# One norm, early modulation products, two projections abreast, later sends and single PSUM banks in a two-layer hybrid backbone kernel

## The chip, the core and the metric

The kernel runs on one core of one Trainium2 chip. The core has five engines: TensorE (PE; its weight loads are listed as PEld), VectorE (DVE), ScalarE (ACT), GpSimd (POOL) and SyncE (SP), which only issues DMAs here; ScalarE issues some as well. Each engine works its own list of instructions in order and waits on semaphores for the others. The metric is the time of the whole program on the core in microseconds, the median of several runs.

## What is computed

The reference runs two layers over a latent stream x (512 tokens of 1024 channels) and a context stream (256 tokens). A layer is, cut to what matters here:

```python
mod = silu(c) @ ada_w[l] + ada_b[l]               # six vectors; c_ctx gives those of the context
h = rmsnorm(x, norm1_w[l]) * (1 + sc1) + sh1      # for both streams
cu, mqkv, mo, mg, aq, ak, av, bg = split(h @ w_in[l])
conv = conformer_conv(cu)                         # width 31, layer norm, projection
m = mlstm_readout(mlstm_bidirectional(mqkv, mg))  # 4 heads of 256, chunkwise, gates in float32
a = attention(aq, ak, av)                         # 8 query heads of 64 on 2 key heads, rotary
x = x + g1 * ((s0 * conv + s1 * m + s2 * a) @ w_out[l])
h = rmsnorm(x, norm2_w[l]) * (1 + sc2) + sh2
x = x + g2 * conv_ffn(h)                          # up, width-3 convolution, gate, down
```

The mLSTM's output is a numerator over max(|denominator|, exp(-m)). The context goes through layer 0 in full; in layer 1 it only gives keys, values and mLSTM states. The output is x, in float32.

## The kernel before

**Layout and products.** Tokens lie along the free dimension, channels on the 128 partitions, so a stream of T = 768 tokens (512 latent, then 256 context) is eight tiles of 128x768. A float32 product is made of three float32r matmuls: each weight block and each activation is split into a high and a low part, and hh·wh, hl·wh, hh·wl are summed in PSUM (accumulate, L664). Weights come as units of four 128x128 blocks in the order of use (class Weights, L188): SP loads a unit into a `raw` tile, ScalarE makes the high part wh (L215), POOL the low part wl (L217); conversions run up to two units ahead, loads five.

**Steps and ticks.** proj (L671) is a generator: one step is one k block of a projection (3 matmuls of 512 columns, and 3 of 256 where the context takes part). A Filler (L234) holds a queue of such generators; run(n) takes n steps from it, and after each step tick counts down the side chains that were handed to chain. A side chain yields a number of ticks that it wants to wait before its next piece is emitted. So the order in each engine's list is written by hand, and gaps in ticks are the distances between the pieces of a chain. drain empties the queue; settle runs the chains out with no steps between.

**The beginning** (L692 to L711). SP loads the eight xt tiles, then aw, the weights of the modulation vectors: ada_first (L436) has four parts of eight 128x512 pieces, (f, vec) with f the half of the channels and vec 1 the scale, 0 the shift. Three parts are loaded at once into buffers that later stages use (`room`), the fourth behind the first product, because its last two pieces take B buffers of the first. For the latent and then the context stream the squares of all eight blocks are summed (Norm.square, L592) and scale_early (L604) makes 1/rms by row sums on PE, a square root on ScalarE, a reciprocal on VectorE, and spreads it over the partitions by PE into PSUM, where VectorE multiplies all eight blocks. Then, for each half, two products (16 matmuls, a copy, four small transposes, an addition), factors (L611), and apply_scaled (L641): ScalarE scales and shifts a block into a t3 tile (a ring of three), VectorE rounds it to the high part hh, and VectorE or POOL takes the low part hl. The first weight unit is taken after all that.

**mLSTM heads** (L1206 to L1249). The gates' projection starts the chain mgates (L760), which ends with PE's L837. Each of four heads queues its projections (conv 16 steps, output gates, the next head's q, k, v: 72 steps) and emits at given steps, listed in HEADS and HEADS1 as `step:what`: D (decay: rows from DRAM, exponentials on ScalarE L1027), S (scores; VectorE multiplies, and denominators, L1058, adds up the columns in L1061), R (normalise, L1074), V (weights times values, L1183), s (split of the finished heads). The digit is the group of 256 queries. R makes row sums on PE (L545), takes Abs on ScalarE, a maximum and a reciprocal on VectorE, and sends the four rows back to all partitions with four DMAs on SP (send_rows, L534); norm_gap ticks later VectorE multiplies six score pieces by them (L1086). head_norm (L1130) sends its rows in the same way. The taps of the width-31 convolution (L924) run on VectorE, one every second step.

**Behind the heads** (L1295 to L1307) two mlstm_out projections are taken six steps far, one after the other, while the last head's chain ends; settle, and then the rest.

**Attention** (L1443 to L1511). Keys, values, one branch gate and three query chunks are queued, 48 steps; prepare(i) (L1377) of a head copies its query (L1383), and finds the maxima of its scores: PE L1396 and L1403 into a pv bank, VectorE L1397 and L1405, then a transpose L1413 and L1414. prepare(0) is chained after 24 steps, the queue is drained, the convolution's output projections and branch gates are queued, and the sweep runs over 64 (layer 0) or 48 (layer 1) items: attend(j) makes a block of scores and its exponentials, weigh(j) multiplies by values. prepare(i + 1) is chained when head i begins.

**PSUM.** Eight banks of 128x512: two mm tiles of 1024 columns (four banks), two sm and two pv tiles of one bank.

## Time and profile before

| | |
|---|---|
| median of 3 runs | 3086.83 us (3085.42 to 3087.39) |
| the profiled execution | 3092.18 us, its span 3090.4 us |
| PE busy | 2839.3 us (92% of the span) |
| PEld, DVE, ACT, POOL busy | 77%, 58%, 38%, 37% |
| mean granted TensorE clock | 0.972 |
| DMA | 262.48 MB, 85 GB/s over the span |
| chain that ended last | PE L668 11% of the span, all else 3% |

A busy share is the time in which an engine executes something. The granted clock is 1.00 at 2.4 GHz and 0.50 at 1.2 GHz; the first 78 us have no record of it and are shown as 1.00. In the lists of waits, a row names the waiting engine and line, then what ended the wait, the sum, how many and the longest. Layer 0 goes to about 1822 us, layer 1 from there.

### The profile page before, as it was taken

The page shows a single profiled execution, that of the slowest core. Times are in us where ns is not written, and L with a number is a line of the kernel's source. Part 1 is how long each engine was busy: PE and PEld are TensorE (multiplying, and loading weights), DVE is VectorE, ACT ScalarE, POOL GpSimd, SP SyncE. Part 2 cuts the span into 40 slices and gives each one's busy share as a digit, 9 for nine tenths or more (in the row PEclk, how much of TensorE's full clock was granted, in tenths as well). Part 3 has the DMA queues.
Part 4 walks back from the last instruction along what each step waited for, and adds up shares of the span by engine and source line. Part 5 has one row for each costly group of instructions (what it writes and reads, how often), then busy time and mean ns, then how long its engine had stood idle before and what let it go on. Part 6 is the DMA issues. An engine that isn't in the chain of part 4 may idle for free. (4 is left out here: it accounts for less than half of the span.)

```text
span 3090.4 us, 42030 instructions
## 1 busy us (share of the span) xinstructions
PE 2839.3 (92%) x15970; PEld 2387.5 (77%) x15970; DVE 1806.4 (58%) x2506; ACT 1164.5 (38%) x2136; POOL 1148.0 (37%) x931
## 2 busy tenths in 40 slices
PE   4999999899899998999999988999989789899999
PEld 2778888788677887888888877887767567777887
DVE  3366776852655335876665565778764663563444
ACT  3333333423444424322322353433434444443333
POOL 1233333323344434333332343334334345444444
PEclk9999999999899998999999989999999999999999
DMA  5454334211111133333333232333322112423333
GB/s 180 149 126 106 60 61 68 49 61 55 31 31 31 56 116 96 113 116 113 113 120 106 71 116 58 68 63 74 69 72 72 35 38 75 153 87 96 93 96 106
DMA packets 156682, 262.48 MB, mean 85 GB/s; under 512 B 17784, under 2 KB 37624, under 8 KB 156480
## 3 DMA queue, kind: packets, MB, share of 16 engines
q1 hardware_dynamic: 150048, 253.28, 29.5%
q10 hardware_dynamic: 6432, 6.52, 0.8%
q8 instruction: 126, 2.06, 0.3%
q14 instruction: 76, 0.62, 0.1%
HBM read 247.05 MB, written 5.46 MB: 82 GB/s over the span
## 5 line engine op out<-in xcount | busy, mean ns | idle before, releaser
L217 POOL TENSOR_TENSOR wl<-raw,wh 128x512 fp32r<-128x512 f32 x659 | 908.4, 1384 | 1516.4 <-ACT wh L215 1444.8
L668 PE MATMUL mm<-hh,wh 128*128 128x512 f32 (+1 forms) x2672 | 965.3, 361 | 21.9 <-ACT wh L215 8.8
L668 PE MATMUL mm<-hh,wl 128*128 128x512 f32 (+1 forms) x2672 | 949.3, 355 | 9.4 <-POOL wl L217 9.4
L668 PE MATMUL mm<-hl,wh 128*128 128x512 f32 (+1 forms) x2672 | 954.9, 357 | 2.0 <-POOL hl L346 1.2
L215 ACT ACTIVATE wh<-raw 128x512 fp32r<-128x512 f32 x662 | 411.1, 625 | 592.7 <-PE mm L668 328.8
L668 PEld LDWEIGHTS mm<-hh,wh 128*128 128x128 f32 x2672 | 513.7, 192 | 120.2 <-issue 23.5
L668 PEld LDWEIGHTS mm<-hh,wl 128*128 128x128 f32 x2672 | 511.5, 191 | 87.9 <-POOL wl L217 14.0
L668 PEld LDWEIGHTS mm<-hl,wh 128*128 128x128 f32 x2672 | 513.4, 192 | 70.8 <-POOL hl L346 1.8
L668 PE MATMUL mm<-C,wh 128*128 128x512 f32 (+1 forms) x1168 | 410.8, 352 | 0.3 <-DVE C L346 0.3
L668 PE MATMUL mm<-B,wh 128*128 128x512 f32 (+1 forms) x976 | 345.5, 354 | 29.2 <-DVE big L1542 15.0
L668 PE MATMUL mm<-B,wl 128*128 128x512 f32 (+1 forms) x976 | 342.9, 351 | 9.9 <-POOL wl L217 9.3
L924 DVE SCALAR_TENSOR_TENSOR AC<-G,par,AC 128x783 f32<-128x783 f32 (+1 forms) x240 | 258.5, 1077 | 3.8
L668 PEld LDWEIGHTS mm<-C,wh 128*128 128x128 f32 x1168 | 227.6, 195 | 28.6 <-DVE C L346 0.5
L668 PEld LDWEIGHTS mm<-B,wh 128*128 128x128 f32 x976 | 190.7, 195 | 61.2 <-ACT wh L215 14.5
L668 PEld LDWEIGHTS mm<-B,wl 128*128 128x128 f32 x976 | 190.1, 195 | 37.8 <-POOL wl L217 14.6
L1592 DVE SCALAR_TENSOR_TENSOR AC<-mm,par,AC 128x511 f32<-128x511 f32 (+1 forms) x132 | 86.7, 657 | 205.1 <-ACT AC L1590 205.1
L1542 DVE SCALAR_TENSOR_TENSOR big<-mm,mod,big 128x512 f32<-128x512 f32 (+1 forms) x144 | 91.1, 657 | 122.9 <-PE mm L668 122.8
L1590 ACT ACTIVATE AC<-mm,par 128x768 f32<-128x768 f32 (+1 forms) x88 | 77.4, 879 | 145.7 <-PE mm L668 145.5
L346 POOL TENSOR_TENSOR P<-t,P 128x512 fp32r<-128x512 f32 (+1 forms) x64 | 73.4, 1148 | 132.3 <-ACT t L1473 75.7
L488 DVE SCALAR_TENSOR_TENSOR P<-C,cs,P 128x512 f32<-128x512 f32 x112 | 114.7, 1056 | 1.5 <-DMA C<-aw 1.5
L1027 ACT ACTIVATE C<-rb,bias 128x128 f32<-128x128 f32 x312 | 96.4, 390 | 35.7 <-DMA rb<-rows 23.2
L1111 PE MATMUL pv<-P,C 128*128 128x256 f32 x624 | 95.9, 291 | 8.0 <-DVE P L346 6.6
(270 smaller groups left out, 3735.8 us busy)
## 6 DMA issues: line engine op xcount, KB each, us to landing
raw<-ws SPq DMA_DIRECT2D x662, 256.0 KB, 2.6
C<-aw SPq DMA_DIRECT2D x104, 256.0 KB, 3.1
big<-aw SPq DMA_DIRECT2D x64, 256.0 KB, 4.2
P<-ws SPq DMA_DIRECT2D x30, 256.0 KB, 2.8
big<-xt SPq DMA_DIRECT2D x16, 384.0 KB, 6.6
rb<-rows ACTq DMA_DIRECT2D x40, 128.0 KB, 4.0
den<-rd SPq DMA_DIRECT2D x80, 64.0 KB, 5.8
B<-aw SPq DMA_DIRECT2D x10, 256.0 KB, 6.5
```

Source lines behind the costliest of these rows:

```text
L215: self.nc.scalar.activation(out=hi, in_=raw, func=AF.Copy)
L217: eng.tensor_tensor(out=lo, in0=raw, in1=hi.bitcast(F32), op=ALU.subtract)
L346: (eng or dve).tensor_tensor(out=out, in0=src, in1=hi.bitcast(F32), op=ALU.subtract)
L488: dve.scalar_tensor_tensor(out=a_, in0=r_, scalar=cs[:, k, q:q + 1], in1=a_, op0=ALU.mult, op1=ALU.add)
L668: pe.matmul(ps[:, o:o + n], w[w_], h[h_][:, so:so + n], start=(k == 0 and i == 0 and o % 512 == 0), stop=(k == n_k - 1 and i == 2), skip_g ...
L924: dve.scalar_tensor_tensor(out=a, in0=t[:, j:j + cw], scalar=par(l, "cw", w0 + j), in1=a, op0=ALU.mult, op1=ALU.add)
L1027: act.activation(out=t[:, off + x * 128:off + x * 128 + 128], in_=rb[:, c0:c0 + 128], func=AF.Exp, bias=bcol(dr, h, key, qb))
L1111: pe.matmul(ps[:, dd * 256:dd * 256 + 256], v_[key // 3][:, vo:vo + 128], b_, start=(ki == 0 and i == 0 and dd == 0), stop=(ki == len(part ...
L1542: dve.scalar_tensor_tensor(out=xs[m][:, o:o + n], in0=ps[:, po:po + n], scalar=gain[:, m, s:s + 1], in1=xs[m][:, o:o + n], op0=ALU.mult, o ...
L1590: act.activation(out=t[:, 0:tq], in_=ps[:, 0:tq], func=AF.Identity, scale=fw(1), bias=fb)
L1592: dve.scalar_tensor_tensor(out=t[:, o + 1:o + n], in0=ps[:, o:o + n - 1], scalar=fw(0), in1=t[:, o + 1:o + n], op0=ALU.mult, op1=ALU.add)
```

## The change

- The beginning: ScalarE takes one dummy square root early. The squares are taken over all 768 columns, and scale_early makes one 1/rms for both streams, spread into an mm tile. All four parts of aw are loaded at the start, the last two pieces into an hh and an hl tile, and three raw units ahead of the fourth part. Two products follow each other before their transposes; the third and fourth are emitted between the blocks of the first half, behind block 1 and 2, and the three raw units are split behind block 3. Blocks are applied one by one, both streams in turn.
- Layer 0's first projections: gates and the first query chunk abreast, a step of each in turn.
- mgates: 1/u is exp(-ln u) on ScalarE instead of a reciprocal on VectorE.
- normalise: no Abs; the maximum with emt and with the negative is taken by VectorE from PSUM. send_gap ticks (2 and 3) pass before the rows are sent, norm_gap is shorter by as much (8 and 11), and every second of the four sends is issued by ScalarE. So does head_norm.
- HEADS1, layer 1's list, has D1 at 4 instead of 13, R0 at 16, S1 at 22, V1 at 61; the last head R0 at 15, S1 at 21, R1 at 35, V0 at 38, V1 and s at 51. HEADS is as it was.
- Three mlstm_out projections instead of two are begun behind layer 1's heads.
- Attention: the convolution's output projections are queued before the sweep, 12 of their steps run before it, prepare(0) and prepare(1) are chained there and prepare(i + 2) at head i; the first maximum comes 5 (layer 0) or 8 (layer 1) ticks after the copy instead of 3, the transpose 3 ticks instead of 2 after the last maximum.
- PSUM: layer 1 has four mm tiles of one bank; a product of 768 columns takes two of them (class Two), and copies out of it are cut at column 512.

```diff
-HEADS1 = [["c o0 o1 q v", "2:S0 13:D1 17:R0 23:S1 39:R1 40:V0 60:D* 62:V1"]] * 3 +     [["c o0 o1 b b x0", "2:S0 13:D1 17:R0 23:S1 39:R1 40:V0 53:s 56:V1"]]
+HEADS1 = [["c o0 o1 q v", "2:S0 4:D1 16:R0 22:S1 39:R1 40:V0 61:V1 61:D*"]] * 3 +     [["c o0 o1 b b x0", "2:S0 4:D1 15:R0 21:S1 35:R1 38:V0 51:V1 51:s"]]
...
-OPT = [dict(COMMON, heads=HEADS, early=1, norm_gap=10, first="g q v",
+OPT = [dict(COMMON, partial=2, heads=HEADS, early=1, first_max=5, send_gap=2, norm_gap=8, first="G v",
...
-       dict(COMMON, heads=HEADS1, early=1, norm_gap=14, first="Q g K v",
+       dict(COMMON, partial=3, heads=HEADS1, early=1, first_max=8, send_gap=3, norm_gap=11, first="Q g K v",
...
+        class Two:
...
+            def __init__(self):
+                self.tiles = mm(512), mm(512)
...
+        def open_banks(l):
+            stack = ExitStack()
+            banks[:] = stack.enter_context(tc.tile_pool(name=f"pm{l}", bufs=2 * l + 2, space=PSUM)), 512 if l else 1024
+            return stack
...
-        def mm():
-            return pp.tile([128, 1024], F32, tag="mm", name=nm("mm"))
+        def mm(w):
+            if w > banks[1]:
+                return Two()
+            return banks[0].tile([128, banks[1]], F32, tag="mm", name=nm("mm"))
...
+        act.activation(out=csg[:, 0, 0:1], in_=eps, func=AF.Sqrt)
...
-                   [lambda w: tgl(w)] * 2 + [lambda w: alloc("sig", 2, w)] * 2 + [lambda w: alloc("rb", 2, w)] * 2 + [tb] * 2
+                   [lambda w: tgl(w)] * 2 + [lambda w: alloc("sig", 2, w)] * 2 + [lambda w: alloc("rb", 2, w)] * 2 + \
+                   [lambda w, t=t: xp.tile([128, T], F32, tag=t, name=nm(t))[:, 0:w] for t in ("hh", "hl")]
...
-                acc, tr, row = pv(), sm(), alloc("den", 1, 512)
+                acc, row = pv(), t3()[:, 0:512] if vec else alloc("den", 1, 512)
...
+                return f, vec, row
+
+            def end(f, vec, row):
+                tr = sm()
...
+            W.load(RAW)
+            load(*parts[3])
             yield
-            product(*parts[0], loaded[0])
-            load(*parts[3])
-            product(*parts[1], loaded[1])
+            a = product(*parts[0], loaded[0])
+            b = product(*parts[1], loaded[1])
+            end(*a)
+            end(*b)
             yield
-            product(*parts[2], loaded[2])
-            product(*parts[3], loaded[3])
+            a = product(*parts[2], loaded[2])
+            yield
+            b = product(*parts[3], loaded[3])
+            end(*a)
+            yield
+            end(*b)
             yield
...
-                sp.dma_start(out=out[:, g * w:g * w + w],
+                (sp, act)[g % 2].dma_start(out=out[:, g * w:g * w + w],
...
+        def abreast(*works):
+
+            for _ in range(KC):
+                for w_ in works:
+                    next(w_)
+                    yield
...
-        for seg in (X, XC):
-            for k in range(KC):
-                norm.square(k, xs[k], seg)
-            norm.scale_early(xs, seg)
+        layer = open_banks(0)
+        for k in range(KC):
+            norm.square(k, xs[k], (0, T, 0))
+        norm.scale_early(xs, (0, T, 0))
         for f in range(2):
             next(first)
             norm.factors(4 * f, 4)
-            for seg in (X, XC):
-                norm.apply_scaled(xs, seg, range(4 * f, 4 * f + 4))
+            for k in range(4 * f, 4 * f + 4):
+                for seg in (X, XC):
+                    norm.apply_scaled(xs, seg, [k])
+                if k == 1:
+                    next(first)
+                elif k == 2:
+                    next(first)
+                elif k == 3:
+                    W.split(RAW)
...
-                dve.reciprocal(u[R, :], u[R, :])
+                act.activation(out=u[R, :], in_=ln[R, :], func=AF.Exp, scale=-1.0)
...
-                act.activation(out=dn, in_=dps[:, 0:128], func=AF.Abs)
-                dve.tensor_tensor(out=dn, in0=dn, in1=emt[:, b0 // 2, :], op=ALU.max)
+                dve.tensor_tensor(out=dn, in0=dps[:, 0:128], in1=emt[:, b0 // 2, :], op=ALU.max)
+                dve.scalar_tensor_tensor(out=dn, in0=dps[:, 0:128], scalar=-1.0, in1=dn, op0=ALU.mult, op1=ALU.max)
                 dve.reciprocal(dn, dn)
+                yield opt["send_gap"]
                 send_rows(acc, dn, 128, h)
...
+            g_ = proj(w_in(tuple(gate)), hs, both, lambda ps: fill.chain(mgates(ps)))
             for what in opt["first"].split():
                 if what == "g":
-                    fill.add(proj(w_in(tuple(gate)), hs, both, lambda ps: fill.chain(mgates(ps))))
+                    fill.add(g_)
+                elif what == "G":
+                    fill.add(abreast(g_, qk_part(0, 0)), *[qk_part(0, i) for i in range(1, 4)])
...
-            og_ = [mlstm_out(0), mlstm_out(1)]
+            og_ = [mlstm_out(m) for m in range(opt["partial"])]
...
-                yield 3
+                yield opt["first_max"]
...
-                    yield 2
+                    yield 3
...
-            fill.run(8)
-            fill.chain(prepare(0))
-            fill.drain()
-
             for m in range(KC):
                 fill.add(branch_out(m, "w_conv_out", ys, 0), bgate())
             fill.add(bgate())
+            fill.run(8)
+            fill.chain(prepare(0))
+            fill.run(10)
+            fill.chain(prepare(1))
+            fill.run(26)
...
-            LEAD, todo = 2, KC * 12
+            LEAD, todo = 2, KC * 12 - 12
...
-                    if it[0] + 1 < AH:
-                        fill.chain(prepare(it[0] + 1))
+                    if it[0] + 2 < AH:
+                        fill.chain(prepare(it[0] + 2))
```

## Rows read from the trace of the kernel before

**Rows 1.** Stages: start:end, length, busy us (instructions) by engine, PEclk, DMA share, GB/s.

```profile
150.00:625.00 475.00, 448.63 (x3022) 389.65 (x3020) 335.46 (x465) 177.15 (x408) 159.80 (x139) 0.98 0.40 80
757.00:836.00 79.00, 64.67 (x370) 51.24 (x369) 59.25 (x73) 41.19 (x61) 28.04 (x20) 0.87 0.10 30
836.00:1010.00 174.00, 160.10 (x845) 129.79 (x844) 93.92 (x137) 86.38 (x174) 73.61 (x66) 1.00 0.11 31
1895.00:2225.00 330.00, 302.81 (x1842) 263.02 (x1841) 244.11 (x345) 130.00 (x303) 130.67 (x112) 0.96 0.34 69
2225.00:2300.00 75.00, 62.64 (x308) 49.75 (x308) 56.64 (x78) 32.09 (x57) 25.96 (x20) 0.91 0.27 64
2360.00:2432.00 72.00, 55.44 (x258) 39.05 (x257) 55.99 (x77) 35.22 (x53) 22.51 (x23) 0.91 0.14 41
2432.00:2561.00 129.00, 109.75 (x468) 82.57 (x467) 83.13 (x122) 57.26 (x104) 53.46 (x43) 1.00 0.12 37
2725.00:3090.40 365.40, 354.02 (x1558) 290.61 (x1556) 168.23 (x202) 134.10 (x216) 164.89 (x128) 1.00 0.32 96
```

**Rows 2.** Timeline, 0 to 76: start, us, engine, line, operation, out<-in, count, [idle before<-releaser].

```profile
14.75 0.66 PE L545 MATMUL sm<-rs,cst 128*32 128x128 f32 x8 [14.75 <-DVE rs L600]
...
32.36 3.64 PE L455 MATMUL pv<-B,cs 128*32 128x512 f32 x16
...
45.26 2.93 ACT L631 ACTIVATE t<-big,mod,amul 128x512 f32<-128x512 f32 x4 [2.23 <-DVE amul L615]
...
47.68 1.39 POOL L346 TENSOR_TENSOR hl<-t,hh 128x512 fp32r<-128x512 f32 x1 [46.66 <-DVE hh L638]
...
73.52 0.80 PE L668 MATMUL mm<-hh,wl 128*128 128x512 f32 x1 [1.75 <-POOL wl L217]
```

**Rows 3.** Stages again: the loads of the beginning, and one group's four sends.

```profile
5.00:35.00 30.00, 8.32 (x64) 5.12 (x64) 15.53 (x30) 9.99 (x19) 0.00 (x0) 1.00 0.96 359
2008.40:2018.60 10.20, 10.20 (x61) 8.98 (x60) 7.22 (x11) 1.71 (x4) 3.26 (x3) 1.00 0.62 69
```

**Rows 4.** Timelines of VectorE and ScalarE in layer 1's gate chain.

```profile
1848.91 4.95 DVE L791 RECIPROCAL C<-C 36x768 f32<-36x768 f32 x1
...
1847.94 0.85 ACT L790 ACTIVATE C<-C 36x768 f32<-36x768 f32 x1
...
1866.49 1.28 ACT L833 ACT_TABLE_LOAD   x1
```

**Rows 5.** Timelines of VectorE, SP and PE in layer 1's head 1.

```profile
2000.99 2.07 DVE L1061 TENSOR_TENSOR den<-den,C 128x256 f32<-128x256 f32 x4
...
2018.54 5.08 DVE L1086 TENSOR_TENSOR C<-C,den 128x512 f32<-128x512 f32 x6 [2.68 <-DMA den<-rd]
...
2008.35 3.84 SPq L537 DMA_DIRECT2D den<-rd  x4
...
2001.75 0.50 PE L668 MATMUL mm<-hh,wh 128*128 128x512 f32 x1 [0.69 <-ACT sig L907]
...
2029.17 1.15 PE L545 MATMUL sm<-den,cst 128*32 128x128 f32 x8 [5.92 <-DVE den L1061]
```

**Rows 6.** Waits: whole span (four rows), then 836:1010 (one) and 2432:2561 (two).

```profile
PE sm L545 <- DVE den L1061: 38.3, 11, 5.9
...
DVE rd L1081 <- ACT rd L1080: 29.8, 12, 5.9
...
DVE C L1086 <- DMA den<-rd: 28.1, 14, 3.4
...
PE sm L837 <- DVE t L822: 11.3, 2, 9.3
...
PE pv L1396 <- ACT C L340: 7.4, 6, 1.2
...
PE pv L1396 <- DVE mx L1397: 7.8, 6, 1.4
PE pv L1396 <- DVE G L1496: 4.7, 4, 1.2
```

More of the change, by code (lines that the diff above doesn't have):

```diff
@@ L299, in build, with __getitem__, stretches @@
         pp = es.enter_context(tc.tile_pool(name="pp", bufs=2, space=PSUM))
+        banks = []
+        class Two:
+            def __init__(self):
+                self.tiles = mm(512), mm(512)
+            def __getitem__(self, at):
+                p_, c_ = at
+                i = c_.start // 512
+                if c_.step == -1:
+                    end = (-1 if c_.stop is None else c_.stop) - 512 * i
+                    return self.tiles[i][p_, slice(c_.start - 512 * i, None if end < 0 else end, -1)]
+                assert c_.stop <= 512 * i + 512
+                return self.tiles[i][p_, c_.start - 512 * i:c_.stop - 512 * i]
+        def open_banks(l):
+            stack = ExitStack()
+            banks[:] = stack.enter_context(tc.tile_pool(name=f"pm{l}", bufs=2 * l + 2, space=PSUM)), 512 if l else 1024
+            return stack
+        def stretches(w):
+            return [(0, w)] if w <= 512 or banks[1] == 1024 else [(0, 512), (512, w)]
         uid = [0]
@@ L671, in proj @@
         def proj(specs, hs, sts, done, segs=None):
-            ps = mm()
+            ps = mm(max(o + n for o, n, _ in sts))
             for k, (spec, h) in enumerate(zip(specs, hs, strict=True)):
@@ L684, in split @@
             hi, lo = make(), make()
-            copy(hi[:, 0:w], src)
-            lo_part(lo[:, 0:w], src, hi[:, 0:w], eng)
+            for a, b in stretches(w):
+                copy(hi[:, a:b], src[:, a:b])
+                lo_part(lo[:, a:b], src[:, a:b], hi[:, a:b], eng)
             return hi, lo
@@ L717, in build @@
             tq = T if wc else L
+            if l:
+                layer = open_banks(l)
             both, own = [X, XC], [X, XC] if wc else [X]
@@ L774, in mgates @@
                 li, z, e, u, ln, lf, ms, g = [tcc() for _ in range(8)]
-                act.activation(out=z[R, :], in_=gp[64:100, 0:T], func=AF.Identity, bias=gb[64:100])
+                for a, b in stretches(T):
+                    act.activation(out=z[R, a:b], in_=gp[64:100, a:b], func=AF.Identity, bias=gb[64:100])
                 for P_, nat, sc in dirs:
@@ L1138, in head_norm @@
                 r = sq[1][:, 0:tq]
+                yield opt["send_gap"]
                 send_rows(r, y, w)
@@ L1300, in build @@
             fill.settle()
-            fill.add(*og_)
+            fill.add(*og_[:2])
             fill.run(4)
             fill.chain(conv_norm())
-            for what in opt["outs"].split():
-                fill.add(bgate() if what == "b" else mlstm_out(int(what)))
+            for m in range(2, KC):
+                fill.add(bgate(), og_[m] if m < len(og_) else mlstm_out(m))
             fill.drain()
@@ L1338, in done @@
                 def done(ps):
-                    copy(av[:, 0:T], ps[:, 0:T])
+                    for a, b in stretches(T):
+                        copy(av[:, a:b], ps[:, a:b])
                     vt.extend([tb(F32R).rearrange("p (b n) -> p b n", n=192) for _ in range(3)])
@@ L1674, in build @@
             assert len(W.blocks) == BLOCKS[l], (l, len(W.blocks))
+            layer.close()
         return plans
```

34 lines of the change are left out of this document (23 added, 11 removed).

## The prediction

> **What bounds the kernel now.** I read the page first, then TensorE's busy time by stage, then who waits for whom, then single stretches. On the page TensorE is busy nearly all the time and no other engine comes near it, so what can be won is its idle time. The stage table [rows 1] says where that lies: in each stretch, the length less PE busy is idle, and a granted clock below 1.00 is time at the lower of the two levels (1.2 instead of 2.4 GHz), in which matmuls take twice as long. Idle: 26.4 us in layer 0's mLSTM heads (150:625), 14.3 and 13.9 in its attention, ahead of and in the sweep over heads (757:836, 836:1010), 27.2 in layer 1's mLSTM heads (1895:2225), 12.4 behind them, 16.6 and 19.3 in its attention (2360:2432, 2432:2561), 11.4 in its feed-forward part. The lower clock costs about (1 - clock) x length x busy share on top: 9 us in 150:625, 8 in 757:836, 12 in 1895:2225, 5 each in 2225:2300 and 2360:2432. The beginning stands before all this: the first matmul that has all its parts runs at 73.52 [rows 2]. The change works in just these stretches, so its worth is the share of their idle time that goes.
>
> **The beginning.** Before [rows 2], the row sums start at 14.75, the first mod product only at 32.36 (3.64 us), behind the norm of the context; ScalarE applies the first half at 45.26. DMA does not set this: the 16 engines are 0.96 busy at 359 GB/s from 5 to 35 [rows 3], and all 12.3 MB (xt, 32 pieces of aw, three raw units) are through at about 5 + 12.3/0.36 = 39 us. In the changed order the three raw loads stand ahead of the last eight aw loads on SP, and none waits for a B buffer any more.
> New order. Squares of 768 columns keep step with the loads, so row sums again start near 15. Sums, one rsqrt and the spreading end near 23 (the two norms' PE steps together, less the table load of 1.28 us [rows 4] that the dummy Sqrt moves ahead). Two products follow on PE at once, 2 x 3.64, then both transposes, 3.8: mods at 34.3, first apply at 34.7 instead of 45.3. The eight 768-wide multiplications on VectorE lie beside the products, so they cost nothing; without that cover they would be 7 us. Behind it three waits queue up: the later products' rows use the ring of three t3 tiles, so block 3 waits for the transposes of product 3 (PE done at 43.3); the weight conversions stand on ScalarE behind block 3 (44.6); the first low weight part stands on POOL behind block 3's low parts (1.39 us for 512 columns [rows 2]), so it is done near 46.6 + 1.3 = 47.9. From there two projections abreast take 3.8 us per k at the lower clock (a 128x512 matmul took 0.80 us at 73.52), and the second half's blocks, from 46.5 at about 2.1 us per k, stay ahead. 73.5 becomes 47.9: **-25** (-20 if POOL or the t3 ring is a block later, -28 if the low part isn't last).
>
> **Gate chain.** VectorE's reciprocal (4.95 us) becomes an exp on ScalarE (ln took 0.85). The trace has a table load between ln and the next exp [rows 4], so I price it at 1.28 + 0.85: the chain is 2.8 us shorter in each layer. PE stood 11.3 us for its end, 9.3 of it in layer 1 [rows 6], and the lower clock follows such a wait. **-6** (0 to -9). The Trainium skill, "ScalarE: Activation LUTs", section "Table sets: the hidden batching unit", has ln followed by exp as one load, since one set holds both. By that the chain would be 1.3 us shorter still in each layer; the load in the row speaks against it.
>
> **mLSTM heads.** The row sums of a group wait for VectorE, 38.3 us in eleven waits, four of them the 5.92 us of layer 1's heads [rows 5, 6], so 14.6 in layer 0. Such a stall is VectorE's work from the normalising multiplications at 2018.54 to the end of the sums, 10.6 us, less what PE has to do meanwhile. The multiplications start 2.68 us late there, since the denominators' rows (four sends, the first at 2008.35) land late: 28.1 us in 14 waits; and in 12 waits VectorE stands 29.8 us for ScalarE's Abs, which comes behind decay exponentials [rows 6]. The change drops the Abs hop for one more small VectorE operation, which brings the denominators 2 to 4 us sooner. In layer 0 (same list of steps) half of 14.6, and a little clock: **-8** (+4 to -16). In layer 1, R0 moves from step 17 to 16, where its sums are not ready: they end at 2003.06 (2000.99 + 2.07), while PE, without the wait of 0.69 us for an accumulator, would ask at 2001.0: a new stall of 2 us. Then the multiplications start on time and R1's stall falls to 3. Net 1 us a head, **-4** (+8 to -22). The last head asks for R1 four steps sooner and keeps its stall, but leaves 5 steps behind V1, and three partial projections instead of two give 6 steps more, at 0.69 us each, where 12.4 us were idle: **-5** (0 to -12).
> Four sends took from 2008.35 to 2018.5, with the DMA engines 0.62 busy [rows 3]; by the row, two queues could bring the last landing forward by a third at most, 3 us. The Trainium skill, "DMA: Bandwidth & Descriptors", section "Issuing engines are not separate DMA queues", says that two issuing engines save issue time only. By that the landing comes about 1 us sooner. The sum holds neither.
> What the sends cost: 52 of 104 go to ScalarE's queue (four took SP 3.84 us, waits included), and wait there for the reciprocal. Behind them stand weight conversions and exponentials; conversions run two units ahead (8 steps, 5.5 us in layer 1), and send_gap gives VectorE 2 or 3 steps. **+2** (0 to +10).
>
> **Attention.** prepare(i) leads by two heads, its first maximum comes 2 (layer 0) or 5 (layer 1) ticks later, and 12 steps of the convolution's output projection move ahead of the sweep. In layer 0's sweep the six waits for the query copy, 7.4 us [rows 6], end within those 2 ticks (about 1.9 us against 1.2): **-7** (-4 to -13). In layer 1's the first maximum waits for the previous head's division (4.7) and the next for VectorE's queue (7.8) [rows 6]; five ticks later neither stands in front, and I take 12 of 19.3: **-12** (-6 to -18). Ahead of the sweep VectorE is the bound in layer 1, 56 of 72 us busy [rows 1]. The 12 steps give 8 us of cover there and 12 in layer 0, but prepare(1) brings its VectorE work, some 6 us, from the sweep. **-8** in layer 0 (0 to -20), **-6** in layer 1 (0 to -15). Where such a stall goes, VectorE's rotary steps are late next.
>
> **Banks.** Layer 1 has four single banks for two double ones. Waits for a free accumulator are 0.69 us per head (counted above) and more than half of the 11.4 us in the feed-forward part: **-5** (-2 to -7). Reopening the pool may make layer 1's first projection wait for layer 0's last residual, and 768-wide copies are cut in two, off the path: **+2** (0 to +4).
>
> **Sum:** -25 -6 -8 -4 -5 +2 -7 -12 -8 -6 -5 +2 = **-82 us**. The profiled execution took 3092.18 us (span 3090.4 and 1.8 around it), so 3010 by it; the median shown is 5.35 lower, and I give 3086.8 - 82 = **3005**.
>
> **Rivals.** *The stalls only move*: VectorE stays the bound in the heads and ahead of both sweeps; the beginning, the gate chain, 10 us of the sweeps and 4 of the banks remain: -45, **3042**. For it: 56 of 72 us. Against: in the sweeps VectorE is busy under two thirds.
> *All waits go*: -25, -9, -38 in the heads, -12 behind them, -64 in attention, -7: -155; two thirds of the way from -82 to there is **2956**.
> *The beginning stays bound by loads*, and only 5 of its 25 us are won: **3025**. For it: 0.96 of the engines; against it: 39 us is well before 47.9.
> *Slower:* ScalarE stands at the sends for the reciprocal. If it comes to each of the 26 groups 10 us too early, PE waits for the part above the 5.5 us of lead: 26 x 4.5 = 117 us, 35 more than the gain: **3122**. It decides from 8.7 us per group. Against it: the Abs that goes stood in the same queue, later than PE's sums by ScalarE's own work.
> *No change*: the edits fall on idle time that others fill; the beginning, a serial chain from the first load to the first projection, speaks against it.
>
> **How the numbers follow.** Forecast 0.60, stalls move 0.20, all go 0.09, loads 0.06, slower 0.03, no change 0.02. A measurement can tell 0.2% (6 us) from none. Faster 0.95, same 0.02, slower 0.03. The range goes from 2970, part way to the case in which all waits go, to 3046, past the one in which stalls move.
>
> **What would show it.** The first matmul with a low weight part near 48 us; no VectorE wait for DMA at the multiplications by denominators; some 2 us of idle before layer 1's R0 sums and 3 before R1's; in the sweeps no wait for the query copy; no wait for sig in layer 1's heads. I am wrong if PE's idle time in the stages of the table falls by less than 35 us, or if weight conversions are late behind ScalarE's sends.

## The result, and the profile after

The changed kernel takes **3042.69 us** (median of four runs, 3039.57 to 3047.87) beside 3087.11 before: ratio 0.9857, 95% interval 0.9843 to 0.9872, so 44 us less. I had given 3005 us, with a range from 2970 to 3046. The sign is right and the range holds the result, but it lies where the rival *the stalls only move* had put it (3042).

The profiled execution took 3040.40 us (span 3038.6), 51.8 less than the profiled one of before; my sum of -82 was made against that one, so 30 us are missing. Both programs issue the same 15970 matmuls, so the start of the n-th one in the two traces tells where the time went. Worked out from the traces:

| up to matmul | stands behind | before, us | after, us | gain so far | in this part | forecast |
|---|---|---|---|---|---|---|
| 250 | the beginning | 92.6 | 62.1 | 30.5 | -30.5 | -25 |
| 500 | layer 0's gates | 134.4 | 108.3 | 26.1 | +4.4 | -3 |
| 4500 | layer 0's heads | 767.3 | 730.3 | 37.0 | -10.9 | -8 |
| 5750 | layer 0's attention | 1028.7 | 994.2 | 34.4 | +2.6 | -15 |
| 9500 | layer 0's rest | 1715.4 | 1679.1 | 36.3 | -1.9 | 0 |
| 10000 | the handover to layer 1 | 1820.4 | 1789.1 | 31.3 | +5.0 | +2 |
| 10250 | layer 1's gates | 1874.9 | 1841.6 | 33.4 | -2.1 | -3 |
| 12250 | layer 1's heads | 2227.5 | 2191.9 | 35.6 | -2.2 | -4 |
| 12750 | the stretch behind them | 2345.1 | 2305.5 | 39.5 | -3.9 | -5 |
| 13750 | layer 1's attention | 2603.6 | 2559.7 | 43.9 | -4.4 | -18 |
| end of the span | the feed-forward part | 3090.4 | 3038.6 | 51.8 | -7.9 | -5 |

The forecast column has the terms of my sum, the gate chain's 6 us shared between the layers; ScalarE's sends, +2, are left out. The two attentions were to bring 33 us and brought 1.8: the 31 us between them are as much as is missing in all, the misses of the other parts cancel.

The stage table of the changed kernel, beside [rows 1]: start:end, length, then busy us and instructions of PE, PEld, DVE, ACT, POOL, granted clock, DMA share, GB/s.

```profile
124.00:588.00 464.00, 442.08 (x3021) 385.38 (x3020) 337.86 (x477) 174.83 (x396) 161.21 (x139) 0.99 0.41 82
720.00:802.00 82.00, 69.46 (x417) 55.63 (x415) 60.75 (x79) 37.27 (x55) 27.32 (x20) 0.92 0.12 36
802.00:976.00 174.00, 156.22 (x799) 125.28 (x799) 92.03 (x132) 87.94 (x177) 73.87 (x67) 0.98 0.10 28
1861.00:2189.00 328.00, 303.69 (x1840) 265.52 (x1840) 249.12 (x363) 128.23 (x303) 126.08 (x112) 0.96 0.34 69
2189.00:2262.00 73.00, 63.44 (x319) 50.23 (x318) 58.90 (x77) 32.04 (x58) 25.73 (x20) 0.93 0.29 69
2326.00:2395.00 69.00, 55.66 (x242) 38.80 (x240) 55.52 (x71) 34.20 (x54) 22.74 (x19) 0.90 0.14 43
2395.00:2517.00 122.00, 106.60 (x446) 79.55 (x447) 83.23 (x122) 54.52 (x100) 51.77 (x40) 0.99 0.12 37
2681.00:3038.60 357.60, 353.15 (x1559) 291.17 (x1557) 167.99 (x202) 133.98 (x217) 164.57 (x128) 1.00 0.34 98
```

Length less PE busy is idle, as before. The feed-forward part fell from 11.4 to 4.5 us. Layer 0's sweep (third row) rose from 13.9 to 17.8, with fewer steps in it; ahead of the sweeps 12.5 and 13.3 us are left of 14.3 and 16.6.

The beginning, from the timeline, beside [rows 2]:

```profile
25.74 2.65 PE L483 MATMUL pv<-C,cs 128*32 128x512 f32 x16
...
28.32 1.05 PE L490 MATMUL sm<-pick,t 128*128 128x2 f32 x8
...
30.58 2.69 ACT L680 ACTIVATE t<-big,mod,amul 128x512 f32<-128x512 f32 x4 [1.43 <-DVE amul L664]
...
42.92 0.80 PE L717 MATMUL mm<-hh,wl 128*128 128x512 f32 x1 [2.12 <-POOL wl L217]
```

The first low weight part is the last thing that PE waits for, as forecast, but at 42.92 instead of 47.9. The first apply stood at 30.58, not 34.7: the second product took 2.65 us, where I had 3.64, and the two transposes took about 1.05 each, where I had 3.8 for the pair.

Who waits, in layer 0's sweep (802:976), then in layer 1's (2395:2517); line waiting, what ended the wait, sum, count, longest:

```profile
PE pv L1565 <- DVE G L1573: 4.4, 2, 2.2
PE pv L1479 <- DVE G L1573: 4.2, 2, 2.3
PE pv L1565 <- DVE B L1573: 2.2, 1, 2.2
PE pv L1479 <- DVE B L1573: 1.9, 1, 1.9
...
PE pv L1472 <- DVE mx L1473: 9.4, 11, 2.0
```

Beside [rows 6]: the six waits for the query copy in layer 0 (7.4 us) are gone, and so are those of layer 1's maxima for the previous head's division (4.7, and 2.4 more; 1.6 us of other waits for it are left there). In their place layer 0 has four kinds of waits for L1573, the division of a head by its denominators, 4.4 + 4.2 + 2.2 + 1.9 = 12.7 us. In layer 1 the wait of one maximum for the reduction of the one before it grew from 7.8 to 9.4. One of layer 0's places, from the timelines of VectorE and PE:

```profile
821.41 0.85 DVE L1573 TENSOR_TENSOR G<-pv,den 64x256 f32<-64x256 f32 x2
...
822.41 0.63 PE L1479 MATMUL pv<-B,C 128*128 128x256 f32 x2 [1.90 <-DVE G L1573]
```

Ahead of layer 0's sweep one wait alone is 6.6 us (waits of PE, 720:802), and VectorE's timeline has the rotary work of a query chunk at that place:

```profile
PE pv L1472 <- DVE mx L1473: 6.9, 2, 6.6
```

```profile
753.48 6.26 DVE L1047 TENSOR_TENSOR t<-G,rb 32x512 f32<-32x512 f32 x4
```

As to the sweep, there are two pv banks. A head's output holds one from its first weighing until the division; all maxima share the other. Before, the last maximum of a coming head, the context's, came ahead of the division in layer 0. Now it comes three ticks later (two more before the first maximum, one more before the transpose), falls into the division, finds both banks held, and PE stands.

The heads, from the waits of PE in layer 1's heads before (1895:2225) and now (1861:2189), then two rows of the whole span, beside [rows 6]:

```profile
PE sm L545 <- DVE den L1061: 23.7, 4, 5.9
...
PE sm L584 <- DVE den L1131: 23.6, 8, 3.6
...
ACT C L1097 <- DMA rb<-rows: 11.2, 14, 2.7
...
DVE C L1157 <- DMA den<-rd: 8.3, 5, 2.8
```

VectorE's wait for the denominators' rows fell from 28.1 to 8.3 us, and its 29.8 us for ScalarE's Abs are gone; PE's wait for VectorE's sums fell only from 38.3 to 31.8, all of it in layer 0's heads (14.6 to 8.2). In layer 1 it is as long as it was; what went there is the waits for a free accumulator, 2.7 us. In layer 1 each head of before waited once, 5.92 us [rows 5]. Now it waits twice, at R0 and at R1 (timeline of PE, head 1):

```profile
1967.24 0.92 PE L584 MATMUL sm<-den,cst 128*32 128x128 f32 x8 [3.11 <-DVE den L1131]
...
1991.88 0.81 PE L584 MATMUL sm<-den,cst 128*32 128x128 f32 x5 [3.44 <-DVE den L1131]
```

And two places where the change costs: the gate chains' ends and the first projection of layer 1 (timeline of PE; before, 2.0 us in layer 0, 9.28 in layer 1 and 2.11):

```profile
92.38 0.78 PE L904 MATMUL sm<-t,cst 36*128 36x120 f32 x2 [3.12 <-DVE t L889]
...
1785.40 0.77 PE L717 MATMUL mm<-hh,wh 128*128 128x512 f32 x1 [7.11 <-DVE big L1619]
...
1835.71 0.56 PE L904 MATMUL sm<-t,cst 36*128 36x120 f32 x1 [8.61 <-DVE t L889]
```

### The profile page after: what moved, and what is told of

Its sections match the earlier page's. It is cut to its first block, busy times and chain, and to the rows that moved or that the text cites. A ratio compares the mean times of both kernels' runs of the same rounds, so it can differ in the third digit from the quotient of the medians.

```text
span 3038.6 us, 42068 instructions
## 1 busy us (share of the span) xinstructions
PE 2827.8 (93%) x15970; PEld 2381.7 (78%) x15970; DVE 1817.7 (60%) x2521; ACT 1156.8 (38%) x2122; POOL 1146.6 (38%) x931
## 5 line engine op out<-in xcount | busy, mean ns | idle before, releaser
L717 PE MATMUL mm<-B,wh 128*128 128x512 f32 (+1 forms) x976 | 344.4, 353 | 24.4 <-DVE big L1619 11.8
L1565 PE MATMUL pv<-P,B 128*128 128x512 f32 (+1 forms) x336 | 94.6, 387 | 12.1 <-DVE G L1573 5.2
```

The source lines that it names most:

```text
L717: pe.matmul(ps[:, o:o + n], w[w_], h[h_][:, so:so + n], start=(k == 0 and i == 0 and o % 512 == 0), stop=(k == n_k - 1 and i == 2), skip_g ...
L1565: pe.matmul(o_[:, 0:n_q], vblock(b, a_)[:, 64 * v_:64 * v_ + 128], b_[:, 0:n_q], start=(ki == 0 and x == 0), stop=(last and x == 2))
```

## The experiments

Twelve kernels; each ratio is to the kernel before, run beside it on the same chip, with its 95% interval. "Against the changed kernel" compares a trace with that of the changed kernel at the same matmul. One caution on such differences: layer 0's heads (matmul 500 to 4500) took from 0.3 to 7.2 us more than in the changed kernel's trace in nine kernels that leave that code as it is, so a difference of a few microseconds there tells nothing.

| kernel | median, us | ratio | interval |
|---|---|---|---|
| the changed kernel | 3042.69 | 0.9857 | 0.9843 to 0.9872 |
| the beginning alone | 3066.70 | 0.9931 | 0.9919 to 0.9943 |
| attention of before | 3052.63 | 0.9885 | 0.9870 to 0.9899 |
| preparation two blocks earlier | 3048.81 | 0.9870 | 0.9857 to 0.9883 |
| banks opened earlier | 3041.12 | 0.9848 | 0.9834 to 0.9862 |
| all sends on SP | 3047.50 | 0.9870 | 0.9853 to 0.9886 |
| Abs on ScalarE again | 3050.26 | 0.9878 | 0.9862 to 0.9895 |
| gates' reciprocal again | 3045.22 | 0.9859 | 0.9839 to 0.9878 |
| first combination | 3034.71 | 0.9828 | 0.9812 to 0.9845 |
| maxima in the single banks | 3029.52 | 0.9804 | 0.9790 to 0.9817 |
| double banks in layer 1 | 3058.89 | 0.9899 | 0.9884 to 0.9913 |
| layer 1's list of before | 3035.37 | 0.9819 | 0.9803 to 0.9836 |
| second combination | 3011.61 | 0.9744 | 0.9729 to 0.9758 |

**The beginning alone.** The kernel before with the diff's hunks on ada_first, scale_early, abreast and the order of the beginning, and in layer 0

```diff
-OPT = [dict(COMMON, heads=HEADS, early=1, norm_gap=10, first="g q v",
+OPT = [dict(COMMON, heads=HEADS, early=1, norm_gap=10, first="G v",
```

> The kernel before with the new beginning alone (one norm for both streams, products early, gates and first query part abreast); all else as before. Theory (the beginning brings 30 us, and the gate chain, which counts steps, takes 4 back): 26 us faster than before, ratio 0.991 to 0.992. Rival (the beginning stays bound by loads): 5 us faster. Rival (the beginning gives all of the 44 us): ratio 0.986.

At matmul 250 it stands where the changed kernel does (62.1 us), and behind layer 0's gates it is 25.7 us ahead of before. By the medians it is 21 us faster, a little less than the theory's 26 and far from either rival. It also has the longer stop at the gates:

```profile
93.87 0.56 PE L873 MATMUL sm<-t,cst 36*128 36x120 f32 x1 [4.57 <-DVE t L858]
```

Before it was 2.0 us. Gates and the first query part abreast leave 32 steps behind the chain's start (three query parts and the values) instead of 40, so PE gets to the chain's end sooner and stands longer: part of the beginning's gain is paid back here.

**The attention of before**, in the changed kernel (fill.run, todo, the chaining of prepare, the ticks):

```diff
-            fill.run(8)
-            fill.chain(prepare(0))
-            fill.run(10)
-            fill.chain(prepare(1))
-            fill.run(26)
...
-                    if it[0] + 2 < AH:
-                        fill.chain(prepare(it[0] + 2))
+                    if it[0] + 1 < AH:
+                        fill.chain(prepare(it[0] + 1))
```

> The changed kernel with the attention's order of before (one head of lead, first maximum after 3 ticks, the 12 steps of the convolution's output back in the sweep). My forecast had 33 us for these edits: by it this run is 33 us slower than the changed kernel, about 3075 us, ratio 0.996. Theory from the two traces (the edits swap a wait for the query copy for one for the head's division, and bring 2 us): 2 us slower than the changed kernel, within 0 to 6, ratio 0.985 to 0.988.

Against the changed kernel its layer 0 attention is 3.2 us shorter and its layer 1 attention 5.2 longer, 2 us in all, as the theory has it. The two other traces with the old attention say the same: in the kernel before and in the beginning alone, layer 0's is 2.6 and 3.5 us shorter and layer 1's 4.3 and 4.5 longer. By the medians' ratios the difference is 0.0028, 9 us, a little outside the theory's range, with intervals that just touch; the forecast's 33 us would be 0.0107. So the edits on attention bring little, and in layer 0 they cost.

**Preparation two key blocks earlier.** Here and in the combinations the chain starts ahead of the head's change:

```diff
-                if j == 0 or it[0] != items[j - 1][0]:
-                    if it[0] + 2 < AH:
-                        fill.chain(prepare(it[0] + 2))
+                at = min(j + 2, len(items) - 1) if j else 0
+                if j == 0 or items[at][0] != items[at - 1][0]:
+                    if items[at][0] + 2 < AH:
+                        fill.chain(prepare(items[at][0] + 2))
```

> The changed kernel with each head's preparation started two key blocks earlier in the sweep, so that its last maximum comes before the head's division, and its copy still has the longer lead. Theory (the maxima were only pushed into the division: 4 us of waits for it per head in layer 0, one in layer 1): no wait for L1573 of the context's maximum or of the first weighing, 10 to 14 us of idle less in layer 0's sweep, 2 to 6 in layer 1's; some 12 us faster than the changed kernel, ratio 0.981 to 0.983. Rival (PE is short of accumulator banks anyway and the waits move to the maxima themselves): no change, ratio 0.986.

The waits of PE for the division in this kernel, in layer 0's sweep (808:975), then in layer 1's (2400:2517):

```profile
PE pv L1479 <- DVE G L1573: 1.9, 1, 1.9
PE pv L1565 <- DVE G L1573: 1.5, 3, 0.8
...
PE pv L1565 <- DVE G L1573: 6.7, 3, 2.7
...
PE pv L1565 <- DVE B L1573: 2.2, 1, 2.2
```

In layer 0 the 12.7 us fell to 3.4, and from matmul 4500 to 5750 the kernel gains 8.5 us on the changed one: the maxima had been pushed into the division. In layer 1 the same edit does the reverse, 8.9 us of waits of the weighings for the division and 7.1 us lost, since a head there has six blocks and the maxima, 8 ticks behind, now begin at the head's change. The sum is no gain, where I had expected 12 us; the median is even 6 us above the changed kernel's, but its trace has 7.2 us more in layer 0's heads, whose code is the same. The time of a maximum counts against the nearest division, not by itself.

**Banks opened earlier.** Layer 1's pool replaces layer 0's ahead of layer 0's last pass, whose 256 columns start at 0 of a tile; two of its accumulators lie in pv:

```diff
+                        if seg == segs[1]:
+                            layer.close()
+                            layer = open_banks(l + 1)
```

> The changed kernel, but layer 1's single banks are opened ahead of layer 0's last pass (the context's), whose first two accumulators lie in two other banks. Theory (the reopened pool makes layer 1's first projection wait for the very last residual, 7.11 us where it was 2.11): the wait falls to 2 us or less, 5 to 7 us faster with the lower clock behind it, ratio 0.983 to 0.984. Rival (the norm that comes behind the residuals is late anyway): the wait moves to the normalised rows, no change.

The same matmul as at 1785.40, from the timeline of this kernel:

```profile
1781.64 0.79 PE L717 MATMUL mm<-hh,wh 128*128 128x512 f32 x1 [0.83 <-ACT wh L215]
```

The 7.11 us are 0.83. From matmul 9500 to 10250 it gains 4.5 us. The medians differ by less than their intervals tell.

**All sends on SP** (send_rows with sp alone).

> The changed kernel with all rows of denominators and norms sent from SP, as before. Theory (a second issuing engine saves issue time alone): one send still takes about 6.3 us to land, VectorE's wait for the denominators (8.3 us in 5 waits in the changed kernel) grows by some 5 us in all, most of it covered; 0 to 3 us slower than the changed kernel, ratio 0.9855 to 0.987. Rival (two queues land a group's rows 3 us sooner): the wait grows to over 25 us and the time by 10 us or more. Rival (ScalarE's issues cost PE the 2 us that I gave them): 2 us faster.

The DMA issues on the page of the changed kernel, then of this one, and this one's waits:

```profile
rb<-rows ACTq DMA_DIRECT2D x40, 128.0 KB, 4.2
den<-rd ACTq DMA_DIRECT2D x40, 64.0 KB, 6.3
```

```profile
den<-rd SPq DMA_DIRECT2D x80, 64.0 KB, 6.3
```

```profile
ACT C L1097 <- DMA rb<-rows: 31.0, 21, 3.8
...
DVE C L1157 <- DMA den<-rd: 16.4, 11, 3.2
```

One send takes 6.3 us to land by either way. The Trainium skill ("DMA: Bandwidth & Descriptors", section "Issuing engines are not separate DMA queues") says that a second issuing engine saves issue time alone; the trace agrees. The wait for the denominators grew by 8.1 us, not by 5, and a wait that I had not named by 20, that of ScalarE's exponentials for the decay rows. ScalarE loads these rows itself in both kernels, with the same median of 4.2 us to landing, so they do not stand behind the sends in SP's queue; why they are waited for longer is not shown. The trace has layer 1's heads 5.0 us longer, where seven other kernels with that code are within 2.4 us of the changed one. The median is 5 us above and by the ratios it is 4, with intervals that overlap. ScalarE's issues cost PE nothing that shows.

**Abs on ScalarE again.**

```diff
-                dve.tensor_tensor(out=dn, in0=dps[:, 0:128], in1=emt[:, b0 // 2, :], op=ALU.max)
-                dve.scalar_tensor_tensor(out=dn, in0=dps[:, 0:128], scalar=-1.0, in1=dn, op0=ALU.mult, op1=ALU.max)
+                act.activation(out=dn, in_=dps[:, 0:128], func=AF.Abs)
+                dve.tensor_tensor(out=dn, in0=dn, in1=emt[:, b0 // 2, :], op=ALU.max)
```

> The changed kernel with the denominators' absolute value on ScalarE again (Abs there, then the maximum on VectorE). Theory (the hop to ScalarE, 29.8 us of VectorE's waits before, is what made the multiplications late): those waits return, with 20 us or more, and 8 us of the heads' 12 are lost, ratio 0.988 to 0.989. Rival (the later sends and the step lists made the gain): 2 us or less, ratio 0.986.

```profile
DVE rd L1151 <- ACT rd L1150: 28.1, 10, 5.7
DVE C L1157 <- DMA den<-rd: 20.1, 8, 4.5
```

Both waits are back, and layer 0's heads are 11.8 us longer than in the changed kernel's trace, more than the 7.2 of chance; in the two other kernels with the Abs, the one before and the beginning alone, they are 10.9 and 10.1 us longer. Layer 1's are 5.4 us shorter. The median is 8 us above, ratio 0.9878, just below what was expected, and the intervals overlap. In layer 0 the hop is the cause; in layer 1 it is not what sets the time.

**The gates' reciprocal again** (`dve.reciprocal(u[R, :], u[R, :])` for the exponential).

> The changed kernel with VectorE's reciprocal in the gate chain again, in place of the exponential on ScalarE. Theory (the 2.7 us that the exponential saves are lost again, since VectorE's next operations then run beside GpSimd's low weight parts and take 1.94 instead of 0.95 us and 3.30 instead of 2.03): waits of PE for the chain of 3.1 and 8.6 us change by less than 1.5 each, and the time by less than 2, ratio 0.985 to 0.987. My forecast had 6 us for it, ratio 0.9877.

PE's two stops at the chain's end are 4.55 and 9.63 us, 1.4 and 1.0 more than in the changed kernel, and the ratio is 0.9859. Why so little, the timelines of VectorE and GpSimd in the changed kernel's layer 1 show:

```profile
1816.60 1.28 ACT L858 ACT_TABLE_LOAD   x1
...
1818.77 0.95 DVE L859 TENSOR_TENSOR C<-C,C 36x768 f32<-36x768 f32 x1 [2.25 <-ACT C L858]
...
1819.34 5.21 POOL L217 TENSOR_TENSOR wl<-raw,wh 128x512 fp32r<-128x512 f32 x3 [3.63 <-ACT wh L215]
...
1819.76 1.94 DVE L861 TENSOR_TENSOR C<-C,C 36x768 f32<-36x768 f32 x1
...
1822.56 3.30 DVE L864 SCALAR_TENSOR_TENSOR C<-C,C 32x512 f32<-32x512 f32 x4
```

and in this kernel:

```profile
1826.19 1.73 DVE L859 TENSOR_TENSOR C<-C,C 36x768 f32<-36x768 f32 x1
...
1827.95 0.95 DVE L861 TENSOR_TENSOR C<-C,C 36x768 f32<-36x768 f32 x1
...
1829.76 2.04 DVE L864 SCALAR_TENSOR_TENSOR C<-C,C 32x512 f32<-32x512 f32 x4
```

The exponential lets VectorE's first product (L859) start 2.8 us earlier, measured from the chain's first operation (at 1807.63 and 1812.22), as I had priced it; and the product itself is 0.78 us shorter, since here a low weight part of GpSimd (1825.81 to 1827.10) runs beside it. But in the changed kernel the operations of L861 and L864 run beside GpSimd's three low weight parts and take 2.25 us longer (0.99 and 1.26). Of the 3.6 us 1.4 are left, and that is about what PE's stops show. The Trainium skill, "SBUF — State Buffer", section "Who interferes with whom", says that a VectorE operation with two inputs from SBUF contends with a GpSimd one that reads SBUF; these rows agree. Of the table load between ln and exp the row at 1816.60 shows 1.28 us, as my sum took it; the Trainium skill's page "ScalarE: Activation LUTs", which the prediction cites, has none there, and the measurement decides.

**First combination.** Banks opened earlier, preparation two blocks earlier in layer 0 and one in layer 1.

> The changed kernel with layer 1's banks opened ahead of the context's last pass, and each head's preparation two key blocks earlier in layer 0's sweep and one in layer 1's. Theory (the handover is worth 4 us and layer 0's earlier preparation 8.6, as the traces of their own runs show; in layer 1 one block earlier moves the waits by no more than 3 either way): 10 to 15 us faster than the changed kernel, ratio 0.981 to 0.9825. Rival (the gain of the earlier preparation is lost to the lower clock or to the next stage): ratio 0.984 or above.

It is 8 us faster than the changed kernel by the medians, 0.9828: better than the rival's 0.984 and just short of the theory's 0.9825, with an interval (0.9812 to 0.9845) that holds both. Layer 1's attention is the same within 0.3 us.

**Maxima in the single banks.** In layer 1 only:

```diff
-                            ps = pv()
+                            ps = mm(512) if l else pv()
```

> The changed kernel, but in layer 1 the scores whose maxima are taken lie in the four single banks of the projections, not in the one bank of pv that the head's output leaves free. Theory (a maximum waits for the one free bank, which the reduction before it gives back: 9.4 us in 11 waits in the sweep, 5.3 and 2.6 in two waits ahead of it): these waits go, 9 to 13 us faster than the changed kernel, ratio 0.9815 to 0.983. Rival (VectorE's queue is the bound, and what waited for a reduction then waits for the rows of maxima or for the parts of the exponentials): 2 us or less, ratio 0.985 to 0.986.

The waits for L1473 in layer 1's sweep are gone altogether; the longest that is left there:

```profile
PE pv L1489 <- DVE mx L1485: 3.1, 4, 1.1
```

From matmul 12750 to 13750 the kernel gains 16.0 us, and the median is 13 us below the changed kernel's, 0.9804 with an interval apart from 0.9843. So in the sweep layer 1's maxima waited for a bank and not for VectorE's time; I had listed that wait under VectorE's queue. Ahead of the sweep 4.8 us in two waits for L1473 are left of 7.9.

**Double banks in layer 1** (`bufs=2`, 1024 columns in both layers, and partial=2).

> The changed kernel with two double banks in layer 1 too (and two partial projections behind its heads instead of three, which need a third accumulator). Theory (single banks bring 6 to 7 us in the feed-forward part and 0.7 per head, and cost 5 at the handover between the layers): 3 to 8 us slower than the changed kernel, the wait at the handover 2.1 us instead of 7.1, waits for sig back in the heads; ratio 0.987 to 0.9885. Rival (the reopening eats all that the banks bring): the same time, ratio 0.986.

It is 16 us slower than the changed kernel by the medians and 13 by the ratios, where I had expected 3 to 8. In the feed-forward part it loses 7.2 us, as thought; behind the heads 6.4, where only two accumulators can be begun. At the handover I was wrong:

```profile
1788.79 0.77 PE L717 MATMUL mm<-hh,wh 128*128 128x512 f32 x1 [7.11 <-DVE big L1619]
```

The wait is the same 7.11 us, with two double banks that are closed and opened again: it is the reopening that costs, whatever the size of the banks, since a new pool waits for the last reader of the old one. The rival fell as well: the banks bring far more than they cost.

**Layer 1's list of before** (HEADS1 alone).

> The changed kernel with the list of steps of layer 1's heads from before. My forecast gave the lists 4 us in the heads and most of 5 behind them: by it 5 to 9 us slower, ratio 0.9875 to 0.9885. Theory from the traces (the heads stay bound by VectorE, whose work per head is the same, and the gain behind them comes from the last head's list): 2 us of it in the heads, 4 behind them, 6 us slower. Rival (a wait that is moved within a head costs what it brought): less than 2 us, ratio 0.986.

The opposite of both: 0.9819 beside 0.9857, with intervals apart, 7 us less by the medians and 12 by the ratios. Its heads (matmul 10250 to 12250) are 12.7 us shorter than the changed kernel's, the stretch behind them is 4.5 longer. In its stage 1871:2186, the same heads, PE's idle time is 15.4 us instead of 24.3, at a granted clock of 0.98 instead of 0.96:

```profile
1871.00:2186.00 315.00, 299.56 (x1846) 263.29 (x1845) 240.72 (x360) 130.19 (x305) 130.50 (x112) 0.98 0.35 73
```

Its two waits in head 1, beside 3.11 and 3.44:

```profile
1975.68 0.38 PE L584 MATMUL sm<-den,cst 128*32 128x128 f32 x2 [0.86 <-DVE den L1131]
...
1998.54 0.38 PE L584 MATMUL sm<-den,cst 128*32 128x128 f32 x2 [2.33 <-DVE den L1131]
```

R0 one step later finds its sums nearly done, so with the other edits the old list is the better one in the heads; the list was taken back as a whole, so which of its entries does it is not shown. The saving does not appear in the whole span of this trace, which lost 10 us in layer 0, whose code is the same. The new list gives most of what they bring there back, and gains only behind the last head.

**Second combination.** Banks opened earlier, preparation two blocks earlier in layer 0 only, layer 1's maxima in the single banks, and

```diff
-            fill.run(10)
+            fill.run(18)
             fill.chain(prepare(1))
-            fill.run(26)
+            fill.run(18)
```

> The earlier opening of layer 1's banks, preparation two key blocks earlier in layer 0's sweep alone, maxima of layer 1 in the single banks, and the second head's preparation 8 steps later ahead of both sweeps. Theory (the parts add: 4, 8.6, 9 to 13, and 2 to 6 ahead of the sweeps, where the maxima stood behind 6.3 us of rotary work on VectorE): 22 to 30 us faster than the changed kernel, ratio 0.976 to 0.979. Rival (VectorE is the bound in layer 1's attention): no better than the earlier combination, ratio 0.982 to 0.983.

It takes **3011.61 us**, 0.9744: the best kernel here, 31 us below the changed one by the medians and 35 by the ratios, more than the theory's 22 to 30. Its trace gains 15.7 us in layer 0's attention, 16.4 in layer 1's and 3.3 at the handover and the gates behind it, which is all of its 35.5. Ahead of and in layer 0's sweep, then in layer 1's:

```profile
720.00:786.00 66.00, 57.99 (x377) 47.38 (x376) 54.29 (x70) 33.20 (x49) 25.96 (x19) 0.95 0.14 41
786.00:960.00 174.00, 161.96 (x841) 130.42 (x840) 96.74 (x141) 91.45 (x179) 77.56 (x68) 0.99 0.11 29
...
2374.00:2481.00 107.00, 100.30 (x437) 77.25 (x436) 81.99 (x118) 53.37 (x98) 50.54 (x40) 1.00 0.15 40
```

The idle time of these stages is 8.0, 12.0 and 6.7 us, where the changed kernel has 12.5, 17.8 and 15.4.

## Why the prediction was right, and where it was wrong

- **Beginning, -25: right, too small.** It is the largest part, and what ends it is the low weight part behind the first blocks, as written. The term was short by 5.5 us. The first apply stands 4.1 us earlier than in my sum: 0.7 come from the norm, 1.3 from the two products, 1.9 from the transposes (3.8 us in my sum, 1.9 in the trace).
- **Gate chain, -6: wrong.** The step that failed is "the chain is 2.8 us shorter in each layer". Up to the end of VectorE's first product it is 3.6 us shorter; what follows gives back 2.25 in layer 1. By the stops of PE, with and without the reciprocal, 1.4 and 1.0 us are left in the two layers. In layer 0 the reordered start left 8 steps fewer to cover the chain, which I had not priced: PE's stop there grew from 2.0 to 3.12 us, and the clock fell behind it, to 0.50 at 96 to 100 us by the stage view. Layer 0's gates cost 4.4 us where I had given them a gain of 3.
- **Heads, -8 and -4: the sums hold, the shares do not.** The Abs hop was the delay that I named, and VectorE's wait for the denominators fell by 20 us; that its return costs time is shown for layer 0 alone. The changed kernel's trace is the fastest of ten there: the nine others with that code are 3.5 us longer on average, so of the 10.9 us some 7 are the change's. In layer 1 the two stalls of a head, 3.11 and 3.44 us where I had 2 and 3, add up to more than the one of before, 5.92. The list of layer 1, which I let cost only "a new stall of 2 us" at R0, costs about 12 us in the heads: with the old list they are 15 us shorter than before, with the new one 2.2.
- **Behind the heads, -5: right** in size (-3.9). With the list of before 4.5 us are lost there, with two accumulators instead of three 6.4; the two are not independent.
- **ScalarE's sends, +2: not seen.** If anything they help: with all sends on SP the kernel is 4 to 5 us slower, with intervals that overlap, and what would make it slower is not shown.
- **Attention, -33 in all: wrong; -1.8.** Three steps failed, and they are the missing 31 us. In layer 0's sweep, "the six waits for the query copy" were to "end within those 2 ticks": they did, but I asked only about the copy and not what the context's maximum, now three ticks later, runs into. In layer 1's, "five ticks later neither stands in front, and I take 12 of 19.3": the wait for the division went, and the other, which I put down to VectorE's queue, was for the one free pv bank. Ahead of the sweeps, "the 12 steps give 8 us of cover there and 12 in layer 0": prepare(1) took the cover, since its maxima stand behind other work on VectorE, 6.6 us in one wait in layer 0 and 5.3 in layer 1; with prepare(1) eight steps later the second combination gains 7 us more in layer 0's attention than the earlier preparation alone. All three are of one kind, and I had it among the rivals as *the stalls only move*, with 0.20. I spoke against it with VectorE's share in the sweeps, under two thirds, which says nothing of a bank.
- **Banks, -5 and reopening +2: right in the net.** -7.9 in the feed-forward part, +5.0 at the handover; the reopening was named, at less than half of its price.
- **The sign of being wrong came true.** "I am wrong if PE's idle time in the stages of the table falls by less than 35 us": by the two stage tables it fell from 141 to 119 us, by 22. The weight conversions, the other sign, are not late: PE's waits for them (whole span) went from 38 to 32 us. Of what was to be seen, the new stalls at R0 and R1 and the end of the waits for the query copy and for sig in layer 1's heads came; the waits for the denominators' rows did not all go.
- **Luck.** The range holds the result because its upper end was set past the rival, and because the misses outside attention cancel: the beginning brought 5.5 us more than forecast, the gates 8 less. The rival's 3042 is met in the number, not in its terms: it gave 6 us to the gate chain and 10 to the sweeps, which brought none of it or little, and nothing to the heads, which brought 13.

The second combination's 79 us are close to the 82 that I had forecast for the change. That is no confirmation of the sum: it takes other edits to get there.

What stays open: why layer 0's heads differ by up to 7 us from trace to trace of the same code; why the exponentials wait longer for the decay rows with all sends on SP; and whether the list of before for three of layer 1's heads, with the new one for the last, adds its gain to the second combination, which was not tried.

## What to carry to other kernels

A stall that is named for the instruction that ended it still has to be asked which resource that instruction held: a reduction that frees the one accumulator looks in the list of waits just like a reduction that is late. When a chain is started earlier or later, look for what it then meets, at both ends: here each shift by some ticks traded a wait for a copy against a wait for a division. And a list of steps that is changed along with what it waits for should be tried unchanged as well: the old one was the better.

## What the runs showed of the hardware

- A two-input operation of VectorE took up to twice its time beside GpSimd's low weight parts: 36x768 in 1.94 us instead of 0.95.
- The landing of a 64 KB send took 6.3 us (median) with all of them on one issuing queue and with half of them on another.
- A stall in layer 1's heads costs more than its own length: the granted clock there was 0.96 with 24.3 us of idle time and 0.98 with 15.4, and of the 12.7 us between the two kernels 8.9 are idle time.
